# Recurrence layers: two products from GpSimd to VectorE, and the split of the output put at places of its own

## The chip, the cores and the metric

The kernel runs on one core of a Trainium2 chip. The metric is device microseconds of one execution. Before the change the median of three runs is 1669.04 us (1668.2 to 1670.75). Names used below: TensorE (PE; PEld is its weight load), VectorE (DVE), ScalarE (ACT), GpSimd (POOL), SyncE (SP, which issues the transfers). SBUF is the on-chip memory that tiles live in, PSUM the banks that matmuls write.

## The reference

One step of a network with four layers over 384 tokens (128 of a prompt, 256 of a sample) with 1024 features. Layers 0 and 3 mix tokens with a gated linear recurrence in both directions, layer 1 with a short gated convolution, layer 2 with pooling; each layer also has an MLP, layer norms and modulation. The part that matters:

```python
def rglru_direction(xc, w_a, b_a, w_x, b_x, lam, h0, reverse):
    xb = xc.reshape(bsz, T, N_LRU_BLOCKS, LRU_BLOCK)
    r = jax.nn.sigmoid(jnp.einsum('btnd,nde->btne', xb, w_a).reshape(bsz, T, D_RNN) + b_a)
    ig = jax.nn.sigmoid(jnp.einsum('btnd,nde->btne', xb, w_x).reshape(bsz, T, D_RNN) + b_x)
    log_a = (-LRU_C * r.astype(jnp.float32)) * jax.nn.softplus(-lam.astype(jnp.float32))
    a = jnp.exp(log_a)
    u = jnp.sqrt(-jnp.expm1(2.0 * log_a)) * (ig * xc).astype(jnp.float32)
    ...
    h, h_last = linear_recurrence(a, u, h0.astype(jnp.float32))      # h[t] = a[t] h[t-1] + u[t]

def lru_mixer(x, w_in, conv_w, conv_b, w_a, b_a, w_x, b_x, lam, w_out, h0):
    gate, rec = jnp.split(x @ w_in, 2, axis=-1)
    xc = depthwise_conv(rec, conv_w, LRU_PAD_L, LRU_PAD_R) + conv_b
    h_f, s_f = rglru_direction(xc, ..., h0[:, 0], False)
    h_b, s_b = rglru_direction(xc, ..., h0[:, 1], True)
    y = jax.nn.gelu(gate) * (h_f + h_b).astype(x.dtype)
    return y @ w_out, jnp.stack([s_f, s_b], axis=1).astype(x.dtype)
```

## The kernel before

**Tiling.** Features lie on the 128 partitions, in 8 chunks, and the tokens on the free axis. A tile of 388 columns is the 384 tokens with gaps between the two groups; 776 columns are both directions of one chunk. Every large product is done in three matmuls for each 128 x 128 tile of weights: weights and inputs are split into a rounded high half (hi, `whi`) and the remainder (lo, `wlo`), and L197, L198 and L199 multiply hi by hi, lo by hi and hi by lo into one PSUM bank (`acc`). Weights arrive as `raw`; ScalarE makes `whi` (L1279) and VectorE `wlo` (L1285), 1024 columns, that is eight tiles, at a time. There are four such pairs of buffers, and a split is made three half blocks ahead.

**Order.** The program is written out as a list of weight tiles. After each tile there is one tick, and `defer(n, fn)` issues a piece of work n ticks later (a tile of three matmuls on TensorE is one tick). From the program written in this order a scheduler of the language then sets the order of each engine's instructions, gives out the eight PSUM banks and the buffers, and adds the waits. Each engine runs its own list strictly in order, so an instruction that waits holds all behind it.

**A recurrence layer.** The input product has 16 output chunks. Eight are the recurrence's: each is convolved by one ScalarE step (L875) and three VectorE steps (L879), all reading the PSUM bank. Eight are the output's gate: ScalarE squares (L993), VectorE makes a polynomial (L996), ScalarE a tanh (L999), VectorE the product (L1000, the last to read the bank). Between them stand four sets of gates, `gates(g)`, for chunks 2g and 2g+1: eight matmuls at full fp32, each in two passes (L893), with a tanh on ScalarE behind each (L895). Behind a set, `chain(g)` defers for its two chunks, each with ticks of its own: `s_p` (VectorE, L916), `s_tau` (two tanh, ScalarE, L930), `s_sqrt` (root on ScalarE, L933, and a product on GpSimd, L934), `s_a` (two exponentials, ScalarE, L941), `s_u` (VectorE L945, then GpSimd fills the gaps, L947 and L948), `s_scan` (two scans on VectorE, L953 and L956), `s_sum` (GpSimd: a fill, the sum of both directions L962, and two copies of the last states, L964 and L965), and `s_y` (VectorE L970, the gated output, then hi on ScalarE, L236, and lo on VectorE, L237). The output product (L197 to L199 on `hid`) takes chunks 0 to 5 first for five of its outputs, and then 6 and 7.

ScalarE's functions come in sets: where root follows tanh or exponential, an `ACT_TABLE_LOAD` stands between.

The names: `hidf` and `lru` are buffers of the chain (a ring of ten for gates, tau and a) and of the layer's scratch, `tmp` a pool of short-lived tiles, `hid` the split halves that the output product reads, `st` the states, `par` the parameters.

Of the kernel before, what the change touches and what calls it, by code (L numbers as in the profile page):

```python
# [11 lines left out]
F32 = mybir.dt.float32  # L12
F32R = mybir.dt.float32r
I32 = mybir.dt.int32
AF = mybir.ActivationFunctionType
ALU = mybir.AluOpType
# [15 lines left out]
LG = 388  # L32
# [98 lines left out]
def backbone_kernel(ctx, tc, xT, par, wmod0, wmodp, wmodv, w1, w2, lin, lgate, lout, scin, scout, poolw, y_out, st_out):  # L131
    nc = tc.nc
    act, vec, gp, pe = nc.scalar, nc.vector, nc.gpsimd, nc.tensor
# [19 lines left out]
    def tmp(n=T):  # L153
        return tmpp.tile([P, LB], F32, tag="tmp", name=nm("tmp"))[:, :n]
# [27 lines left out]
    def defer(n, fn):  # L182
        seq[0] += 1
        heapq.heappush(heap, (tickno[0] + n, seq[0], fn))
# [50 lines left out]
    def split_hi_lo(src, hi, lo, on_lo=None):  # L235
        act.activation(hi, src, AF.Copy)  # L236
        (on_lo or vec).tensor_tensor(lo, src, hi.bitcast(F32), op=ALU.subtract)  # L237
# [39 lines left out]
    def lru_col(t, j, c, d):  # L277
        i = (j * C + c) * 2 + d
        return t[:, i : i + 1]
# [567 lines left out]
    def lru(l, j, ng):  # L847
        S = {}
# [15 lines left out]
        def buf():  # L864
            ring[0] += 1
            return S["ring"][ring[0] % len(S["ring"])][:, : 2 * LG]
# [18 lines left out]
        def gates(g):  # L885
            def make(i):
                c, d, k = 2 * g + i // 4, (i // 2) % 2, i % 2

                def f(w):
                    if i % 4 == 0:  # L890
                        S["tr", c], S["ti", c] = buf(), buf()
                    ps = acc()[:, :LG]
                    pe.matmul(ps, lhsT=w, rhs=S["xc", c], start=True, stop=True)  # L893
                    dst = S[("tr", "ti")[k], c][:, d * LG : (d + 1) * LG]
                    act.activation(dst, ps, AF.Tanh, scale=0.5, bias=lru_col((bah, bxh)[k], j, c, d))  # L895
                    if i == 7:
                        chain(g)

                return f

            def block(raw):
                for i in range(8):
                    make(i)(raw[:, i * P : (i + 1) * P])
                    if i < 7:
                        tick()

            G(lgate[j, g], block)

        def chain(g):
            ca, cb = 2 * g, 2 * g + 1  # L910
            two = lambda t: t.rearrange("p (d t) -> p d t", d=2)
            gap = lambda t: two(t)[:, :, TP : TP + 3]

            def s_p(c):
                ti = S["ti", c]
                vec.scalar_tensor_tensor(  # L916
                    two(ti),
                    two(ti),
                    1.0,
                    S["xc", c].unsqueeze(1).to_broadcast([P, 2, LG]),  # L920
                    op0=ALU.add,
                    op1=ALU.mult,
                )

            def s_tau(c):
                S["tau", c] = buf()
                for d in range(2):
                    s = slice(d * LG, (d + 1) * LG)
                    cq = lru_col(c8q, j, c, d)
                    act.activation(S["tau", c][:, s], S["tr", c][:, s], AF.Tanh, scale=cq, bias=cq)  # L930

            def s_sqrt(c):
                act.activation(S["tau", c], S["tau", c], AF.Sqrt, scale=0.25)  # L933
                gp.tensor_tensor(S["ti", c], S["ti", c], S["tau", c], op=ALU.mult)  # L934

            def s_a(c):
                S["a", c] = buf()
                for d in range(2):
                    s = slice(d * LG, (d + 1) * LG)
                    ch = lru_col(c8h, j, c, d)  # L940
                    act.activation(S["a", c][:, s], S["tr", c][:, s], AF.Exp, scale=ch, bias=ch)  # L941

            def s_u(c):
                a, u = S["a", c], S["ti", c]
                vec.scalar_tensor_tensor(u, a, 1.0, u, op0=ALU.add, op1=ALU.mult)  # L945
                e = PCOLS["edge"][0] + (j * C + c) * 6
                gp.memset(gap(a), 0.0)  # L947
                gp.tensor_copy(gap(u), two(par_t[:, e : e + 6]))  # L948

            def s_scan(c):  # L950
                a, u, h = S["a", c], S["ti", c], S["tr", c]
                n = LG - 1
                vec.tensor_tensor_scan(h[:, :n], a[:, :n], u[:, :n], 0.0, op0=ALU.mult, op1=ALU.add)  # L953
                hb = PCOLS["h0b"][0] + j * C + c
                rev = lambda t: t[:, LG : LG + n][:, ::-1]
                vec.tensor_tensor_scan(rev(h), rev(a), rev(u), par_t[:, hb : hb + 1], op0=ALU.mult, op1=ALU.add)  # L956

            def s_sum(c):
                h = S["tr", c]
                hs = tmp(LG)  # L960
                gp.memset(hs[:, LG - 1 :], 0.0)
                gp.tensor_tensor(hs[:, : LG - 1], h[:, : LG - 1], h[:, LG : 2 * LG - 1], op=ALU.add)  # L962
                i = j * 16 + c
                gp.tensor_copy(st[:, i : i + 1], h[:, TP - 1 : TP])  # L964
                gp.tensor_copy(st[:, i + 8 : i + 9], h[:, LG : LG + 1])  # L965
                S["hs", c] = hs

            def s_y(c):
                gg = S["gg", c]
                vec.scalar_tensor_tensor(gg, gg, 0.5, S["hs", c], op0=ALU.mult, op1=ALU.mult)  # L970
                hi, lo = S["y"][c]
                split_hi_lo(gg, hi, lo)

            for fn, da, db in (
                (s_p, 1, 2),
                (s_tau, 1, 3),
                (s_sqrt, 6, 6),
                (s_a, 10, 12),
                (s_u, 16, 18),
                (s_scan, 17, 19),  # L980
                (s_sum, 18, 20),
                (s_y, 22, 25),
            ):
                defer(da, lambda fn=fn: fn(ca))
                defer(db, lambda fn=fn: fn(cb))
# [306 lines left out]
    for it in items:  # L1292
# [14 lines left out]
        else:  # L1307
# [9 lines left out]
            hi, lo = wt[k]  # L1317
# [144 lines left out]
```

## Time and profile before

| | |
|---|---|
| median of 3 runs | 1669.04 us (1668.2 to 1670.75) |
| profiled execution, its own time | 1668.76 us |
| its span in the trace | 1667.0 us |
| mean granted clock of TensorE | 0.984 |
| first recurrence layer with its tail | 57 to 186 us of the span |
| second recurrence layer with its tail | 1249 to 1376 us of the span |

The rest of the execution's time over the span, 1.8 us, lies around it. A row of the timeline gives the start in us from the span's start, the time that the instruction or group took, the engine, the line, the operation, out<-in with shapes, how many were joined, and in brackets the idle time of that engine before the row and what ended it. A row of stretches gives its bounds and length, the busy time of PE, PEld, DVE, ACT and POOL with counts, the granted clock (1 is full), the DMA share and GB/s. The lines themselves stand with the prediction.

### The profile page before, as it was taken

What the parts mean: (1) busy time and instruction counts of PE and PEld (TensorE: products, weight loads), DVE (VectorE), ACT (ScalarE), POOL (GpSimd) and SP (SyncE); (2) the same over time, 40 slices, a digit from 0 to 9 for tenths busy, and PEclk for the clock granted to TensorE, in tenths of its full rate; (3) what the DMA queues carried; (4) which work ended last, traced back from release to release, by engine and by line L of the source; (5) the groups of instructions that cost most, each with busy time, mean ns of one, the idle gap of its engine ahead of it and who ended that gap; (6) DMA issues with size and microseconds to landing.
All of it is one profiled execution on the core that took longest, in us unless ns stands there. A gap on an engine that the chain in (4) does not pass through costs nothing.

```text
span 1667.0 us, 24422 instructions
## 1 busy us (share of the span) xinstructions
PE 1592.4 (96%) x9656; PEld 1507.4 (90%) x9656; DVE 1179.3 (71%) x1790; ACT 746.4 (45%) x1128; POOL 409.9 (25%) x477
## 2 busy tenths in 40 slices
PE   7989999999999999999996899999999889999996
PEld 6667899999999999999995699999988789999995
DVE  4777999787475569867647899687477888534544
ACT  3775652243353345324434553244259746423432
POOL 2235350002320046000055250000433354000043
PEclk9999999999999999999998999999999999999998
DMA  9767356556443535654533356556333343333321
GB/s 372 266 233 273 130 202 251 182 179 247 152 152 127 192 137 202 227 177 175 213 143 127 127 202 230 200 190 235 107 115 101 129 162 127 127 127 127 127 76 38
DMA packets 42163, 287.75 MB, mean 173 GB/s; under 512 B 4801, under 2 KB 6977, under 8 KB 8129
## 3 DMA queue, kind: packets, MB, share of 16 engines
q1 hardware_dynamic: 42048, 286.20, 48.0%
q8 instruction: 75, 1.23, 0.3%
q14 instruction: 40, 0.32, 0.1%
HBM read 284.59 MB, written 1.59 MB: 172 GB/s over the span
## 4 chain that ended last, share of the span: by engine, by line
PE 80%; DVE 10%; ACT 4%; POOL 2%; issue 2%; DMA 1%; SPq 0%; DVEq 0%; POOLq 0%; ACTq 0%
PE acc L197 26%; PE acc L199 25%; PE acc L198 25%; DVE wlo L1285 1%; ACT hidf L930 1%; DVE lru L879 1%; PE acc L453 1%; DMA raw<-in_wmod 1%; POOL tmp L962 1%; DVE hidf L945 1%; DVE X L570 1%; PE acc L893 1%; DVE hidf L956 1%; ACT hidf L933 1%; ACT L933 1%
## 5 line engine op out<-in xcount | busy, mean ns | idle before, releaser
L1285 DVE TENSOR_TENSOR wlo<-raw,whi 128x1024 fp32r<-128x1024 f32 x338 | 436.5, 1292 | 170.5 <-ACT whi L1279 169.3
L1279 ACT ACTIVATE whi<-raw 128x1024 fp32r<-128x1024 f32 x338 | 356.2, 1056 | 427.9 <-PE acc L199 351.2
L197 PE MATMUL acc<-h,whi 128*128 128x384 f32 (+2 forms) x1488 | 508.5, 342 | 18.4 <-ACT h L718 10.5
L198 PE MATMUL acc<-h,wlo 128*128 128x384 f32 (+2 forms) x1488 | 506.1, 340 | 0.0
L199 PE MATMUL acc<-h,whi 128*128 128x384 f32 (+2 forms) x1488 | 477.4, 341 | 3.2 <-POOL h L723 3.2
L197 PE MATMUL acc<-hid,whi 128*128 128x384 f32 (+1 forms) x1216 | 413.9, 340 | 3.1 <-ACT hid L236 3.1
L199 PE MATMUL acc<-hid,whi 128*128 128x384 f32 (+1 forms) x1216 | 410.8, 338 | 3.3 <-DVE hid L237 3.3
L198 PE MATMUL acc<-hid,wlo 128*128 128x384 f32 (+1 forms) x1216 | 409.9, 337 | 0.0
L197 PEld LDWEIGHTS acc<-h,whi 128*128 128x128 f32 x1488 | 281.9, 189 | 29.7 <-ACT h L718 11.6
L199 PEld LDWEIGHTS acc<-h,whi 128*128 128x128 f32 x1488 | 278.8, 189 | 6.4 <-POOL h L723 4.9
L198 PEld LDWEIGHTS acc<-h,wlo 128*128 128x128 f32 x1488 | 281.6, 189 | 1.5 <-issue 0.5
L197 PEld LDWEIGHTS acc<-hid,whi 128*128 128x128 f32 x1216 | 229.1, 188 | 8.3 <-ACT hid L236 4.3
L199 PEld LDWEIGHTS acc<-hid,whi 128*128 128x128 f32 x1216 | 229.1, 188 | 4.6 <-DVE hid L237 4.6
L198 PEld LDWEIGHTS acc<-hid,wlo 128*128 128x128 f32 x1216 | 228.9, 188 | 0.9
L830 ACT ACTIVATE tmp<-acc,par 128x384 f32<-128x384 f32 x128 | 74.2, 580 | 259.3 <-PE acc L199 259.3
L570 POOL TENSOR_TENSOR X<-X,ssb 128x384 f32<-128x384 f32 x49 | 55.7, 1172 | 484.3 <-ACT ssb L568 484.3
L547 DVE SCALAR_TENSOR_TENSOR X<-acc,m,X 128x128 f32<-128x128 f32 (+1 forms) x176 | 64.5, 410 | 127.1 <-PE acc L199 127.1
L446 DVE SCALAR_TENSOR_TENSOR mac<-macr,sil,mac 128x512 f32<-128x512 f32 x176 | 125.5, 747 | 0.0
L832 DVE TENSOR_TENSOR tmp<-tmp 128x384 f32<-128x384 f32 x128 | 71.7, 560 | 65.9 <-ACT tmp L830 65.8
L446 DVE SCALAR_TENSOR_TENSOR mac<-mac,sil 128x512 f32<-128x512 f32 x132 | 94.6, 752 | 0.0
L777 POOL TENSOR_SCALAR X<-X,ag,xbb 128x128 f32<-128x128 f32 x64 | 91.8, 1448 | 0.4
L420 POOL TENSOR_SCALAR sc<-m 128x16 f32<-128x16 f32 x7 | 3.5, 496 | 335.8 <-DVE m L384 335.4
(193 smaller groups left out, 1343.6 us busy)
## 6 DMA issues: line engine op xcount, KB each, us to landing
raw<-in_w SPq DMA_DIRECT2D x128, 1024.0 KB, 4.8
raw<-in_wmodp SPq DMA_DIRECT2D x26, 1024.0 KB, 4.9
macr<-in_wmodv SPq DMA_DIRECT2D x22, 1024.0 KB, 5.1
mac<-in_wmodv SPq DMA_DIRECT2D x22, 1024.0 KB, 4.9
park<-in_wmodp SPq DMA_DIRECT2D x18, 1024.0 KB, 8.2
raw<-in_lin SPq DMA_DIRECT2D x16, 1024.0 KB, 5.2
raw<-in_scin SPq DMA_DIRECT2D x12, 1024.0 KB, 4.8
raw<-in_wmod SPq DMA_DIRECT2D x8, 1024.0 KB, 7.4
```

Source lines behind the costliest of these rows:

```text
L197: pe.matmul(ps, lhsT=hi, rhs=xhi, start=first, stop=False)
L198: pe.matmul(ps, lhsT=lo, rhs=xhi, start=False, stop=False)
L199: late = lambda: pe.matmul(ps, lhsT=hi, rhs=xlo, start=False, stop=last)
L446: vec.scalar_tensor_tensor(a, x, w, a, op0=ALU.mult, op1=ALU.add)
L547: vec.scalar_tensor_tensor(Xt[c][:, o : o + n], ps[:, a:b], col(g, c, k), Xt[c][:, o : o + n], op0=ALU.mult, op1=ALU.add)
L570: (vec if fast and i > 2 else gp).tensor_tensor(Xt[i], Xt[i], ssb, op=ALU.subtract)
L777: gp.tensor_scalar(Xt[c][:, a:b], Xt[c][:, a:b], col(g, c, k), col(xb, c, k), op0=ALU.mult, op1=ALU.add)
L830: act.activation(r, ps[:, :T], AF.Relu, bias=par_t[:, i : i + 1])
L832: vec.tensor_tensor(q, r, r, op=ALU.mult)
L933: act.activation(S["tau", c], S["tau", c], AF.Sqrt, scale=0.25)
L1279: act.activation(hi, raws[id(raw)][:, i * 1024 : (i + 1) * 1024], AF.Copy)
L1285: vec.tensor_tensor(lo, raws[id(raw)][:, i * 1024 : (i + 1) * 1024], hi.bitcast(F32), op=ALU.subtract)
```

## The change

The product behind the root (L934) moves from GpSimd to VectorE and becomes a step of its own, `s_mul`, at ticks 12 and 14 for the two chunks; before it was issued right behind the root at tick 6. The sum of the two directions (L962) moves to VectorE. The exponentials go from ticks 10 and 12 to 9 and 11, `s_u` and `s_scan` to 17 and 21, `s_sum` and `s_y` to 18 and 22. Hi (`s_hi`) and lo (`s_lo`) of the output become steps of their own, four and six ticks behind `s_y`.

```diff
             def s_sqrt(c):
                 act.activation(S["tau", c], S["tau", c], AF.Sqrt, scale=0.25)
-                gp.tensor_tensor(S["ti", c], S["ti", c], S["tau", c], op=ALU.mult)
+
+            def s_mul(c):
+                vec.tensor_tensor(S["ti", c], S["ti", c], S["tau", c], op=ALU.mult)
...
-                gp.tensor_tensor(hs[:, : LG - 1], h[:, : LG - 1], h[:, LG : 2 * LG - 1], op=ALU.add)
+                vec.tensor_tensor(hs[:, : LG - 1], h[:, : LG - 1], h[:, LG : 2 * LG - 1], op=ALU.add)
...
                 vec.scalar_tensor_tensor(gg, gg, 0.5, S["hs", c], op0=ALU.mult, op1=ALU.mult)
+
+            def s_hi(c):
+                act.activation(S["y"][c][0], S["gg", c], AF.Copy)
+
+            def s_lo(c):
                 hi, lo = S["y"][c]
-                split_hi_lo(gg, hi, lo)
+                vec.tensor_tensor(lo, S["gg", c], hi.bitcast(F32), op=ALU.subtract)
...
                 (s_sqrt, 6, 6),
-                (s_a, 10, 12),
-                (s_u, 16, 18),
-                (s_scan, 17, 19),
-                (s_sum, 18, 20),
-                (s_y, 22, 25),
+                (s_a, 9, 11),
+                (s_mul, 12, 14),
+                (s_u, 17, 21),
+                (s_scan, 17, 21),
+                (s_sum, 18, 22),
+                (s_y, 18, 22),
+                (s_hi, 22, 26),
+                (s_lo, 24, 28),
```

Lines of the changed kernel: the product is L936, the exponentials L943, `s_u` L947 with its fills L949 and L950, the scans L955 and L958, the sum L964 with its copies L966 and L967, y L972, hi L975, lo L979; the gate of the output is L1003, L1006, L1009 and L1010, the splits of weights L1289 and L1295.

TensorE's and SyncE's lists keep their order; only VectorE's, ScalarE's and GpSimd's lists of the two recurrence layers differ. Three places. First, VectorE in the first layer, at the chain of the second set of gates (`acc_970` is the bank of a gate chunk, whose last reader is L1000 or L1010). Before, from the first `s_u` of this set:

```order
L945 SCALAR_TENSOR_TENSOR hidf_135<-hidf_140,hidf_135 128x776
L879 SCALAR_TENSOR_TENSOR lru_134<-acc_919,par,lru_134 128x388
L953 SCALAR_TENSOR_TENSOR lru_134<-hidf_140,hidf_135 128x387
L879 SCALAR_TENSOR_TENSOR lru_134<-acc_919,par,lru_134 128x388
L956 SCALAR_TENSOR_TENSOR lru_134<-hidf_140,par,hidf_135 128x387
L879 SCALAR_TENSOR_TENSOR lru_134<-acc_919,par,lru_134 128x388
L945 SCALAR_TENSOR_TENSOR hidf_137<-hidf_141,hidf_137 128x776
L1285 TENSOR_TENSOR wlo_980<-raw_820,whi_979 128x1024
L953 SCALAR_TENSOR_TENSOR hidf_136<-hidf_141,hidf_137 128x387
L956 SCALAR_TENSOR_TENSOR hidf_136<-hidf_141,par,hidf_137 128x387
L996 SCALAR_TENSOR_TENSOR tmp_1016<-tmp_1016,acc_970 128x388
L970 SCALAR_TENSOR_TENSOR lru_134<-lru_134,tmp_1008 128x388
```

Now, in the same place, behind the product L936, a lo, the L947 and the two scans of chunk 2g+1, which now come first:

```order
L879 SCALAR_TENSOR_TENSOR lru_134<-acc_919,par,lru_134 128x388 x3
L936 TENSOR_TENSOR hidf_135<-hidf_135,hidf_138 128x776
L1295 TENSOR_TENSOR wlo_979<-raw_820,whi_978 128x1024
L947 SCALAR_TENSOR_TENSOR hidf_135<-hidf_140,hidf_135 128x776
L1006 SCALAR_TENSOR_TENSOR tmp_1014<-tmp_1014,acc_970 128x388
L955 SCALAR_TENSOR_TENSOR lru_134<-hidf_140,hidf_135 128x387
L958 SCALAR_TENSOR_TENSOR lru_134<-hidf_140,par,hidf_135 128x387
L964 TENSOR_TENSOR tmp_1041<-hidf_136 128x387
L964 TENSOR_TENSOR tmp_1005<-lru_134 128x387
L972 SCALAR_TENSOR_TENSOR lru_134<-lru_134,tmp_1041 128x388
L972 SCALAR_TENSOR_TENSOR lru_134<-lru_134,tmp_1005 128x388
L1010 SCALAR_TENSOR_TENSOR lru_134<-tmp_1015,acc_970 128x388
```

The two chunks have changed places, both products and both sums have come in, one weight split and the lo's stand elsewhere.

Second, ScalarE at the same place (`hidf_138` and `hidf_139` are tau of the two chunks). Before:

```order
L933 ACT_TABLE_LOAD
L933 ACTIVATE hidf_138<-hidf_138 128x776
L933 ACTIVATE hidf_139<-hidf_139 128x776
L875 ACTIVATE lru_134<-acc_919,par 128x388
L941 ACT_TABLE_LOAD
```

Now:

```order
L933 ACT_TABLE_LOAD
L933 ACTIVATE hidf_139<-hidf_139 128x776
L975 ACTIVATE hid_127<-lru_134 128x388
L930 ACT_TABLE_LOAD
L930 ACTIVATE hidf_138<-lru_134,c8q 128x388 x2
L875 ACTIVATE lru_134<-acc_919,par 128x388
L933 ACT_TABLE_LOAD
L933 ACTIVATE hidf_138<-hidf_138 128x776
```

The two roots, side by side before, have the tanh of the first chunk between them now, with two more table loads. It is the only set where this happens.

Third, VectorE at the tail of the first layer, chunks 6 and 7 (`hid_132` and `hid_133`). Before:

```order
L945 SCALAR_TENSOR_TENSOR lru_134<-hidf_137,lru_134 128x776
L1285 TENSOR_TENSOR wlo_1446<-raw_1273,whi_1445 128x1024
L953 SCALAR_TENSOR_TENSOR hidf_142<-hidf_137,lru_134 128x387
L956 SCALAR_TENSOR_TENSOR hidf_142<-hidf_137,par,lru_134 128x387
L970 SCALAR_TENSOR_TENSOR lru_134<-lru_134,tmp_1435 128x388
L1285 TENSOR_TENSOR wlo_1490<-raw_1273,whi_1489 128x1024
L237 TENSOR_TENSOR hid_132<-lru_134,hid_132 128x388
L970 SCALAR_TENSOR_TENSOR lru_134<-lru_134,tmp_1451 128x388
L1285 TENSOR_TENSOR wlo_1522<-raw_1313,whi_1521 128x1024
L237 TENSOR_TENSOR hid_133<-lru_134,hid_133 128x388
```

Now:

```order
L947 SCALAR_TENSOR_TENSOR lru_134<-hidf_137,lru_134 128x776
L972 SCALAR_TENSOR_TENSOR lru_134<-lru_134,tmp_1432 128x388
L955 SCALAR_TENSOR_TENSOR hidf_142<-hidf_137,lru_134 128x387
L958 SCALAR_TENSOR_TENSOR hidf_142<-hidf_137,par,lru_134 128x387
L1295 TENSOR_TENSOR wlo_1442<-raw_1274,whi_1441 128x1024
L964 TENSOR_TENSOR tmp_1460<-hidf_142 128x387
L979 TENSOR_TENSOR hid_132<-lru_134,hid_132 128x388
L972 SCALAR_TENSOR_TENSOR lru_134<-lru_134,tmp_1460 128x388
L1295 TENSOR_TENSOR wlo_1489<-raw_1274,whi_1488 128x1024
L979 TENSOR_TENSOR hid_133<-lru_134,hid_133 128x388
```

The y of chunk 6 stands ahead of the scans of chunk 7, and its lo ahead of chunk 7's y; the sum L964 has come in, and one of the three weight splits stands further up.

## The prediction

> **What bounds the kernel now.** I read the page first, then the busy time of the first recurrence layer, then the idle times of TensorE, then what VectorE, GpSimd and ScalarE did ahead of each.
>
> ```profile
> PE 1592.4 (96%) x9656; PEld 1507.4 (90%) x9656; DVE 1179.3 (71%) x1790; ACT 746.4 (45%) x1128; POOL 409.9 (25%) x477
> PE 80%; DVE 10%; ACT 4%; POOL 2%; issue 2%; DMA 1%; SPq 0%; DVEq 0%; POOLq 0%; ACTq 0%
> 57.00:186.00 129.00, 116.61 (x693) 92.42 (x696) 98.22 (x140) 86.38 (x132) 52.63 (x68) 0.97 0.64 233
> ```
>
> TensorE is the bound. The last row is the first recurrence layer (stretch, length, busy time of PE, PEld, DVE, ACT, POOL, granted clock): of 129 us TensorE is idle 12.4, and VectorE has only 31 free. The change can only win back idle time and lowered clock in the two such layers, and adds work to the engine that is nearly full there. The idle time sits in a few places; in the first layer in two.
>
> Place 1, the third set of gates (two TensorE rows, then a row of the stretch behind, with the granted clock third from its end):
>
> ```profile
> 99.92 3.53 PE L893 MATMUL acc<-lru,raw 128*128 128x388 f32 x10
> 107.66 3.50 PE L893 MATMUL acc<-lru,raw 128*128 128x388 f32 x6 [4.21 <-DVE lru L1000]
> 108.00:112.00 4.00, 4.00 (x18) 1.63 (x20) 3.94 (x8) 4.00 (x9) 0.00 (x0) 0.57 0.43 104
> ```
>
> A gate is two passes, so the first row is five gates. The sixth needs the PSUM bank that L1000 on VectorE reads last, and waits 4.21 us; the clock then drops. Why is L1000 late? VectorE, GpSimd and ScalarE:
>
> ```profile
> 93.54 2.60 DVE L945 SCALAR_TENSOR_TENSOR hidf<-hidf,hidf 128x776 f32<-128x776 f32 x1 [2.51 <-POOL hidf L934]
> 96.07 0.61 DVE L879 SCALAR_TENSOR_TENSOR lru<-acc,par,lru 128x388 f32<-128x388 f32 x1
> 96.60 0.95 DVE L953 TENSOR_TENSOR_SCAN lru<-hidf,hidf 128x387 f32<-128x387 f32 x1
> 97.47 0.59 DVE L879 SCALAR_TENSOR_TENSOR lru<-acc,par,lru 128x388 f32<-128x388 f32 x1
> ...
> 105.45 1.21 DVE L1285 TENSOR_TENSOR wlo<-raw,whi 128x1024 fp32r<-128x1024 f32 x1
> 106.58 0.55 DVE L237 TENSOR_TENSOR hid<-lru,hid 128x388 fp32r<-128x388 f32 x1
> 107.06 0.54 DVE L1000 SCALAR_TENSOR_TENSOR lru<-tmp,acc 128x388 f32<-128x388 f32 x1
> ```
> ```profile
> 91.61 3.71 POOL L934 TENSOR_TENSOR hidf<-hidf,hidf 128x776 f32<-128x776 f32 x2 [5.94 <-ACT hidf L933]
> ```
> ```profile
> 89.39 1.28 ACT L933 ACT_TABLE_LOAD   x1
> 90.68 1.59 ACT L933 ACTIVATE hidf<-hidf 128x776 f32<-128x776 f32 x2
> 104.50 0.53 ACT L999 ACTIVATE tmp<-tmp 128x388 f32<-128x388 f32 x1 [6.76 <-DVE tmp L996]
> ```
>
> VectorE stands 2.51 us for the product on GpSimd, then its own L945 takes 2.60 us while GpSimd's second product runs; alone the same form takes 0.94 (row at 149.75 below). From 93.54 on VectorE is never free, and ScalarE waits 6.76 us for it.
>
> Place 2, the tail: the output product needs hi and lo of the last two chunks.
>
> ```profile
> 155.98 0.44 PE L197 MATMUL acc<-hid,whi 128*128 128x388 f32 x1 [1.24 <-ACT hid L236]
> 157.84 0.44 PE L199 MATMUL acc<-hid,whi 128*128 128x388 f32 x1 [1.24 <-DVE hid L237]
> 158.87 0.44 PE L197 MATMUL acc<-hid,whi 128*128 128x388 f32 x1 [0.59 <-ACT hid L236]
> 159.92 0.69 PE L199 MATMUL acc<-hid,whi 128*128 128x388 f32 x1 [0.43 <-DVE hid L237]
> 160.00:164.00 4.00, 4.00 (x13) 3.56 (x14) 1.97 (x3) 1.50 (x2) 0.00 (x0) 0.62 1.01 414
> 149.75 0.94 DVE L945 SCALAR_TENSOR_TENSOR lru<-hidf,lru 128x776 f32<-128x776 f32 x1
> 153.03 0.96 DVE L953 TENSOR_TENSOR_SCAN hidf<-hidf,lru 128x387 f32<-128x387 f32 x1 [1.21 <-POOL lru L948]
> 149.91 2.80 POOL L962 TENSOR_TENSOR tmp<-hidf 128x387 f32<-128x387 f32 x1
> 155.40 0.53 ACT L236 ACTIVATE hid<-lru 128x388 fp32r<-128x388 f32 x1 [5.57 <-DVE lru L970]
> ```
>
> The sum L962 on GpSimd takes 2.80 us beside VectorE, holds up the fill L948 behind it, and so the scan.
>
> The second recurrence layer has the same pattern, at four sets and the tail:
>
> ```profile
> 1275.72 0.45 PE L197 MATMUL acc<-h,whi 128*128 128x392 f32 x1 [0.97 <-DVE lru L1000]
> 1293.38 2.85 PE L893 MATMUL acc<-lru,raw 128*128 128x388 f32 x8 [0.23 <-issue]
> 1298.18 2.19 PE L893 MATMUL acc<-lru,raw 128*128 128x388 f32 x6 [1.95 <-DVE lru L879]
> 1301.64 0.92 PE L893 MATMUL acc<-lru,raw 128*128 128x388 f32 x2 [1.27 <-ACT lru L895]
> 1303.95 0.70 PE L197 MATMUL acc<-h,whi 128*128 128x392 f32 x1 [1.39 <-ACT hidf L895]
> 1323.23 2.87 PE L893 MATMUL acc<-lru,raw 128*128 128x388 f32 x8 [0.83 <-DVE lru L879]
> 1302.00:1310.00 8.00, 6.61 (x21) 6.05 (x20) 6.86 (x11) 7.93 (x15) 0.00 (x0) 0.57 0.66 216
> 1284.26 1.59 ACT L933 ACTIVATE hidf<-hidf 128x776 f32<-128x776 f32 x2
> 1287.10 2.60 DVE L945 SCALAR_TENSOR_TENSOR hidf<-hidf,hidf 128x776 f32<-128x776 f32 x1 [5.12 <-POOL hidf L934]
> 1347.02 0.44 PE L197 MATMUL acc<-hid,whi 128*128 128x388 f32 x1 [0.71 <-ACT hid L236]
> 1348.88 0.44 PE L199 MATMUL acc<-hid,whi 128*128 128x388 f32 x1 [1.24 <-DVE hid L237]
> 1351.00:1355.00 4.00, 4.00 (x12) 3.56 (x13) 1.97 (x3) 1.35 (x2) 0.00 (x0) 0.58 0.40 158
> ```
>
> **The change, part by part.** The product L934 as it stands on GpSimd (form, count, busy time, mean ns, idle time before):
>
> ```profile
> L934 POOL TENSOR_TENSOR hidf<-hidf,hidf 128x776 f32<-128x776 f32 x10 | 18.5, 1869 | 54.5 <-ACT hidf L933 54.5
> ```
>
> GpSimd loses 16 of these and 16 of L962. VectorE has no row of the 776-wide product; between the 388-wide L237 (start to next start 0.48) and the 1024-wide L1285 (1.13), both products of two SBUF operands, a line gives 0.88; the ends 0.48 and 1.22 bound it. The sum is as wide as L237: 0.48. So VectorE takes on 16 x 1.36 = 21.8 us over the two layers, 2.7 per set of gates. It loses the stretching: L945 drops from 2.60 to 0.94 where GpSimd's product ran beside it, and the waits for GpSimd of 2.51 and 5.12 go.
>
> Contention does not vanish: GpSimd keeps fills and state copies. [...]
>
> Place 1. The compiled order changes: the root of the set's second chunk comes first on ScalarE, then a rounding, then a table load, two tanh, a conv start and a second table load before the other root: two loads more in the program, here only. The first root ends between 89.8 and 91.5 (before: 90.68 plus half of 1.59); I take 90.6. The second: 0.43 + 1.28 + 1.2 + 0.56 + 1.28 + 0.8 = 5.5 later, 96.1. VectorE from 90.6 to the end of the gate's last step (L1010, formerly L1000): two products 1.76, two of the old L945 1.76, four scans 3.6, three conv steps 1.6, one split 1.13, and two sums, two y, one lo, one poly, one L1010 at 0.47 each, 3.3: 13.1 us. The second product is reached at 96.2, so its root costs nothing; 0.4 goes on GpSimd's fill before the first scan. That is 104.1, with hand-offs at most 105.5; I take 105.0 against 107.60. Gain 2.6, and if the clock holds, (1 - 0.57) x 4 = 1.7 more: 4.3 (from 0 to 5.3). The loads run on ScalarE beside VectorE's backlog.
>
> [...]
>
> Place 2. Hi and lo now stand at separate ticks, and the scan no longer waits for L962 and its fill. In the old time scale the last scan starts at 149.75 + 0.85 (L947) + 0.47 (y) = 151.1, and behind it stand two scans 1.8, split 1.13, sum, lo, y at 0.47, split 1.13, lo 0.55: the last lo at 157.1, the last hi at 156.0. TensorE without stalls wants them at 156.4 and 155.8. Chunk 6 is ready long before. The fill behind L947 costs nothing, since the y stands between. Left: 0.7 of 3.5, gain 2.8 (1 to 3.5), and the clock's (1 - 0.62) x 4 = 1.5 (0 to 1.5). First layer: -8.6.
>
> Second layer. Second set: the 0.97 goes, since L945's stretch ahead of L1000 goes. Third set: the roots begin at 1284.26 now, and with the 0.97 and a lighter queue ahead of them the first ends at about 1283.5. VectorE then has, up to the last of the six conv steps (L879) that this set waits for, two products 1.76, one old L945 0.88, the fill 0.35, two scans 1.8, six conv steps 3.2, a split 1.13, a sum and a y 0.96: 10.1, that is 1293.6. The second half of the set wants it at 1293.38 - 1.0 + 2.85 = 1295.2, so the 1.95 goes and the two waits behind it with it: sixteen passes of 0.345 from 1293.38 end at 1298.9 instead of 1303.95, 5.0. Clock: (1 - 0.57) x 8 = 3.4, less as TensorE stood 1.4 of the stretch; 3.0. Fourth set: VectorE is late in turn. From 1283.5 some 18 us of its work stand before this set's chain can go on (to 1301), and ScalarE's rounding of chunk 5, which waits for a y in that queue, stands ahead of the last two tanh, and so of the next roots. I get waits of 0.9 and 1.85 where 0.83 was: +1.9 (0 to 4, with a lost clock). Tail: with the last two waits as in the first layer it loses 0.71 + 1.24 + 0.59 + 0.43 = 3.0; VectorE being later here, I leave 1.4: 1.6 gained, and (1 - 0.58) x 4 = 1.7. Together 1.0 + 5.0 + 3.0 - 1.9 + 1.6 + 1.7 = 10.4.
>
> Edits at no cost: the exponentials, one tick earlier, run in ScalarE's free time. The weight splits (L1285) stand behind more VectorE work, but are made three half blocks ahead, and the product that reads the low half never waits now:
>
> ```profile
> L198 PE MATMUL acc<-h,wlo 128*128 128x384 f32 (+2 forms) x1488 | 506.1, 340 | 0.0
> ```
>
> That cover would be gone if VectorE fell some 10 us behind. SP's transfers keep their order. GpSimd's fills and copies now stand behind nothing long. Other layers are unchanged.
>
> Sum: 8.6 + 10.4 = 19.0 off the profiled execution's 1668.76 (0.28 under the median of 1669.04): 1649.8. I say **1650**.
>
> **Rivals.**
> A, part of it. The clock stays low at the third set of the second layer (+3.0) and falls at its fourth, where 2.75 us of waits come close together (+2 to +3), or place 1's L1010 stays near 107: 1655 to 1661. For it: place 2 lost its clock after 3.5 us of scattered waits. [...]
> B, only the tails gain (2.8 + 1.5 + 1.6 + 1.7 = 7.6): 1661. Needs VectorE's new 2.7 per set to use up all that the stretch gives back.
> C, the change does not do what it says: rounding set later keeps the output waiting as before and the new waits cancel the gates' gain: about 1668. Against it: in the compiled order chunk 6's lo stands ahead of chunk 7's y.
> D, slower. VectorE becomes the gate: no relief from GpSimd's remaining copies, and 2.7 us of new work lie ahead of the conv steps and L1010 at three sets, 8.1, plus the two loads 2.6: 1679. It decides if the old L945 still takes above 1.4 us and L1010 ends after 107.6.
>
> **How the numbers follow.** Forecast 0.62 (own range 1644 to 1655), A 0.22, B 0.05, C 0.05, D 0.06. The range 1644 to 1661 leaves out C, D and a little of both ends. 0.2% (3.3 us) is what a measurement of this kernel can tell from no change. Faster 0.89, same 0.05, slower 0.06.
>
> **What would show it.** Right: the old L945 at 0.95 everywhere; the third set of the first layer with a wait near 1.6 and no clock under 1; at the tail one wait of some 0.7; the second layer's third set without a wait over 0.5. Wrong: ScalarE's roundings (L975) standing for VectorE ahead of the tanh of the gates, or conv steps (L879) releasing the gates late in more than the fourth set.

## The result, and the profile after

| | before | after |
|---|---|---|
| median of 4 runs each | 1669.22 us (1668.2 to 1670.75) | 1649.66 us (1649.31 to 1650.79) |
| profiled execution, its own time | 1668.76 | 1649.62 |
| its span | 1667.0 | 1647.8 |
| mean granted clock | 0.984 | 0.989 |

The ratio is 0.9882 with a 95% interval of 0.9869 to 0.9894: 1.2% faster, 19.6 us. The forecast was 1650.

The page of the changed kernel, busy times and chain:

```profile
PE 1583.4 (96%) x9656; PEld 1501.8 (91%) x9656; DVE 1188.8 (72%) x1822; ACT 749.8 (46%) x1130; POOL 362.7 (22%) x445
PE 80%; DVE 12%; ACT 4%; issue 2%; POOL 1%; DMA 1%; SPq 0%; DVEq 0%; POOLq 0%; ACTq 0%
```

GpSimd has 47 us less, but VectorE has only 9.5 us more, although rows of 24.3 us came to it (16 of L936 with 15.4 in sum, 16 of L964 with 8.9). In part its other rows got shorter: L945's sixteen take 15.4 us in sum where they took 21.5, the y's 2.4 less and the weight splits 2.8 less. In part it is counting: rows that follow one another directly overlap by some 0.09 us in the records, and the busy time counts that once. TensorE's busy time fell by 9.0 with the same instructions; by an estimate from the two clocks, 0.989 of full speed over the span instead of 0.984, about 8 of it go with the granted clock (0.005 of 1592.4). The two recurrence layers as stretches (bounds as before, moved with the work):

```profile
55.00:179.00 124.00, 117.93 (x722) 93.41 (x725) 107.33 (x166) 92.29 (x138) 29.64 (x52) 0.99 0.67 249
1240.00:1357.00 117.00, 109.88 (x558) 96.97 (x560) 104.55 (x149) 91.53 (x141) 25.68 (x49) 1.00 0.39 140
```

VectorE is now busy 107 of 124 and 105 of 117 us, GpSimd less than 30. By lines, the moved product (L936) and the old L945 (L947 now), and the sum (L964) on VectorE:

```profile
L936 DVE TENSOR_TENSOR hidf<-hidf,hidf 128x776 f32<-128x776 f32 x10 | 9.4, 962 | 7.6 <-ACT hidf L933 7.6
L947 DVE SCALAR_TENSOR_TENSOR hidf<-hidf,hidf 128x776 f32<-128x776 f32 x10 | 9.6, 964 | 5.4 <-ACT hidf L943 5.4
L964 DVE TENSOR_TENSOR tmp<-hidf 128x387 f32<-128x387 f32 x12 | 6.6, 553 | 0.0
```

The product takes 0.96 us here and 1.87 on GpSimd. L947 takes 0.964 on average where L945 took 1.501, with the same shape and inputs. It waits for the exponentials only; no wait for GpSimd is left in it. Over the two layers VectorE's waits for GpSimd fall from 10.6 to 1.2 us. GpSimd's one-column copies of the last states still read SBUF beside VectorE. They take 0.18 us at the least and up to 2.52, while none of VectorE's L936 and L947 takes more than 0.97; the forecast's sum has no term for them.

Places 1 and 2 of the prediction, TensorE:

```profile
102.23 4.18 PE L893 MATMUL acc<-lru,raw 128*128 128x388 f32 x12
106.79 1.90 PE L893 MATMUL acc<-lru,raw 128*128 128x388 f32 x4 [0.38 <-DVE lru L1010]
...
152.50 0.44 PE L197 MATMUL acc<-hid,whi 128*128 128x388 f32 x1 [0.30 <-ACT hid L975]
153.55 0.44 PE L199 MATMUL acc<-hid,whi 128*128 128x388 f32 x1 [0.44 <-DVE hid L979]
```

The 4.21 us has become 0.38, and the tail's four waits (3.5 us) two of 0.74 together. The clock stays at 1 behind both:

```profile
106.00:110.00 4.00, 3.56 (x24) 1.40 (x23) 4.00 (x8) 3.70 (x9) 0.37 (x3) 1.00 0.67 225
152.00:156.00 4.00, 2.89 (x14) 1.96 (x12) 4.00 (x6) 1.51 (x2) 0.00 (x0) 1.00 0.48 131
```

The second layer:

```profile
1260.91 5.38 PE L893 MATMUL acc<-lru,raw 128*128 128x388 f32 x16
1283.29 5.38 PE L893 MATMUL acc<-lru,raw 128*128 128x388 f32 x16
1303.05 2.85 PE L893 MATMUL acc<-lru,raw 128*128 128x388 f32 x8 [1.51 <-ACT whi L1289]
1307.59 2.87 PE L893 MATMUL acc<-lru,raw 128*128 128x388 f32 x8 [1.69 <-DVE lru L879]
...
1331.72 0.45 PE L197 MATMUL acc<-hid,whi 128*128 128x388 f32 x1 [0.53 <-ACT hid L975]
1332.77 0.45 PE L199 MATMUL acc<-hid,whi 128*128 128x388 f32 x1 [0.42 <-DVE hid L979]
```

The second and third sets run through. The fourth has two new waits. The first of them is put down to a split of weights on ScalarE; VectorE's rows show what really came last:

```profile
1297.79 0.97 DVE L936 TENSOR_TENSOR lru<-lru,hidf 128x776 f32<-128x776 f32 x1 [1.01 <-ACT hidf L933]
1298.67 0.96 DVE L936 TENSOR_TENSOR hidf<-hidf,hidf 128x776 f32<-128x776 f32 x1
...
1302.36 0.60 DVE L879 SCALAR_TENSOR_TENSOR lru<-acc,par,lru 128x388 f32<-128x388 f32 x1
```

The third conv step of the chunk ends at 1302.96, and the gates that read its result start at 1303.05.

Where the 19.2 us between the two spans lie, by the starts of the same matmuls in both traces (after minus before, then the step from the line above):

| place | after - before | step |
|---|---|---|
| first product of layer 0 (44.40, 45.49) | +1.09 | +1.09 |
| second set of gates (76.59, 79.38) | +2.79 | +1.70 |
| third set (99.92, 102.23) | +2.31 | -0.48 |
| fourth set (128.93, 126.05) | -2.88 | -5.19 |
| behind the first tail (188.92, 181.70) | -7.22 | -4.34 |
| first set of layer 3 (1250.29, 1241.81) | -8.48 | -1.26 |
| third set of layer 3 (1293.38, 1283.29) | -10.09 | -1.61 |
| its fourth set (1319.63, 1303.05) | -16.58 | -6.49 |
| behind its tail (1372.48, 1353.34) | -19.14 | -2.56 |

Some of these steps do not come from the change. The first 1.09 begins with the first transfer, for which the first matmul waits 9.74 us instead of 8.44. The 1.70 behind it is a difference of clock behind a wait that is the same in both: 1.84 us for L879, with a clock of 1.00 behind it in before and of 0.50 for 3.41 us in after. The -1.26 lies in layers whose code is the same. In the traces of this case (that with the fills left out) the first product of layer 0 starts between 44.4 and 47.3 us, and the stretch from behind the first tail to the first set of layer 3 takes 1060.0 to 1062.9, so a difference of 2 us between two executions need not come from an edit.

```profile
63.08 2.85 PE L893 MATMUL acc<-lru,raw 128*128 128x388 f32 x8 [1.84 <-DVE lru L879]
```
```profile
64.18 4.54 PE L893 MATMUL acc<-lru,raw 128*128 128x388 f32 x8 [1.84 <-DVE lru L879]
```

### The profile page after: what moved, and what is told of

The parts are those of the page before. It is cut to its first block, busy times and chain, and to the rows that moved or that the text cites. A ratio compares the mean times of both kernels' runs of the same rounds, so it can differ in the third digit from the quotient of the medians.

```text
span 1647.8 us, 24431 instructions
## 1 busy us (share of the span) xinstructions
PE 1583.4 (96%) x9656; PEld 1501.8 (91%) x9656; DVE 1188.8 (72%) x1822; ACT 749.8 (46%) x1130; POOL 362.7 (22%) x445
## 4 chain that ended last, share of the span: by engine, by line
PE 80%; DVE 12%; ACT 4%; issue 2%; POOL 1%; DMA 1%; SPq 0%; DVEq 0%; POOLq 0%; ACTq 0%
PE acc L197 26%; PE acc L199 25%; PE acc L198 25%; DVE wlo L1295 2%; DVE lru L879 1%; DMA raw<-in_wmod 1%; ACT hidf L930 1%; PE acc L453 1%; DVE X L570 1%; DVE hidf L958 1%; DVE X L547 1%; ACT L933 1%; ACT hidf L933 1%; DVE X L659 1%; POOL h L723 1%
## 5 line engine op out<-in xcount | busy, mean ns | idle before, releaser
L1295 DVE TENSOR_TENSOR wlo<-raw,whi 128x1024 fp32r<-128x1024 f32 x338 | 433.7, 1284 | 168.0 <-ACT whi L1289 166.7
L1289 ACT ACTIVATE whi<-raw 128x1024 fp32r<-128x1024 f32 x338 | 356.1, 1056 | 428.1 <-PE acc L199 351.7
L197 PE MATMUL acc<-h,whi 128*128 128x384 f32 (+2 forms) x1488 | 507.6, 341 | 16.0 <-ACT h L718 10.5
```

Source lines behind the costliest of these rows:

```text
L197: pe.matmul(ps, lhsT=hi, rhs=xhi, start=first, stop=False)
L1289: act.activation(hi, raws[id(raw)][:, i * 1024 : (i + 1) * 1024], AF.Copy)
L1295: vec.tensor_tensor(lo, raws[id(raw)][:, i * 1024 : (i + 1) * 1024], hi.bitcast(F32), op=ALU.subtract)
```

## The experiments

The question was which part of the change makes the gain and by what mechanism. Theory M: taking the products off GpSimd does it, because GpSimd's instructions stretch VectorE's beside them and because VectorE waits for GpSimd's results. Rival P: the new places do it. All kernels below were timed against before; the ratio and interval are against before's runs on the same chip.

| kernel | median us | ratio to before, 95% |
|---|---|---|
| both products moved, old places | 1654.74 | 0.991 (0.9896 to 0.9923) |
| new places, both products on GpSimd | 1669.28 | 0.9999 (0.9991 to 1.0008) |
| whole change, product on GpSimd | 1660.18 | 0.9938 (0.9924 to 0.9951) |
| whole change, sum on GpSimd | 1663.31 | 0.9967 (0.9954 to 0.9979) |
| whole change, and an unused product on GpSimd | 1662.18 | 0.9957 (0.9945 to 0.9969) |
| whole change, and an unused sum on GpSimd | 1664.42 | 0.9967 (0.9958 to 0.9977) |
| both moved, old places, hi and lo later | 1653.13 | 0.9904 (0.9891 to 0.9917) |
| whole change, hi and lo at y | 1654.21 | 0.991 (0.9895 to 0.9925) |
| sum on GpSimd, hi and lo later still | 1665.21 | 0.9969 (0.9957 to 0.9981) |
| whole change, hi and lo two ticks earlier | 1651.61 | 0.9893 (0.988 to 0.9907) |
| whole change, conv of chunk 1 earlier | 1648.42 | 0.9876 (0.9863 to 0.989) |
| whole change, fills on GpSimd | 1654.27 | 0.9914 (0.9899 to 0.9929) |

**Only the engines.** Before, with two words changed and every step at its old place.

```diff
-                gp.tensor_tensor(S["ti", c], S["ti", c], S["tau", c], op=ALU.mult)
+                vec.tensor_tensor(S["ti", c], S["ti", c], S["tau", c], op=ALU.mult)
...
-                gp.tensor_tensor(hs[:, : LG - 1], h[:, : LG - 1], h[:, LG : 2 * LG - 1], op=ALU.add)
+                vec.tensor_tensor(hs[:, : LG - 1], h[:, : LG - 1], h[:, LG : 2 * LG - 1], op=ALU.add)
```

> Both products on VectorE, but every step at its old place, hi and lo right behind y. Theory M (the gain comes from taking the products off GpSimd: the waits for L934, the stretch of L945 beside it, and the fill that waits behind L962): the gates of the third sets gain nearly as in the whole change, the tails about half: 1652 to 1657 us. Rival P (the gain comes from the new places; the moves alone only load VectorE): 1664 us or more.

1654.7 us: 14.2 of the 19.6 us, as M said. All sixteen rows of L945 take 0.94 to 0.97 us, at their old places. The second layer's fourth set pays for it in this version, with a wait of 4.00, behind which eight passes take 5.54 us where 2.85 is usual:

```profile
1311.01 5.54 PE L893 MATMUL acc<-lru,raw 128*128 128x388 f32 x8 [4.00 <-DVE lru L879]
```

**Only the places.** The whole change with both products on GpSimd (`gp` in both lines).

> All the new places, but both products stay on GpSimd. M: the product comes six ticks later on GpSimd and still stretches VectorE, so the gates' waits stay or grow; only the tails can gain: 1661 to 1670 us. P: 1650 to 1656 us.

1669.3 us: no change at all. Waits moved: the tail of the first layer still waits 2.53 us for hi, and the second layer's fourth set starts with a wait of 4.85. P falls.

```profile
160.95 0.45 PE L197 MATMUL acc<-hid,whi 128*128 128x388 f32 x1 [2.53 <-ACT hid L975]
...
1320.62 8.03 PE L893 MATMUL acc<-lru,raw 128*128 128x388 f32 x16 [4.85 <-ACT tmp L1003]
```

**One product at a time.** The whole change with one of the two `vec` lines back on `gp`.

> The whole change, but the product behind the root stays on GpSimd (at its new ticks 12 and 14). M: the wait for it and the stretch of the old L945 come back, the tails keep their gain: 1657 to 1665 us. P: 1650 to 1653 us.

> The whole change, but the sum of the directions stays on GpSimd. M: the gates keep their gain and the tails lose about half, as the fill for the last scan stands behind the sum again and y waits for the sum: 1652 to 1656 us. P: 1649 to 1651 us. If VectorE's load were what limits the changed kernel, taking 7.7 us off it would make it faster: under 1648 us.

The product back on GpSimd costs 10.5 us, inside M's range. The sum back costs 13.7, far more than either theory said. It was expected to matter at the tails alone, and a VectorE with less to do did not make the kernel faster either. With the product back, VectorE waits 7.5 us in all for it, and L947 takes up to 2.59 us again. With the sum back, the trace shows it holding the gates too: ScalarE's tanh L930 waits 4.37 us for it at the fourth set of the first layer, since it writes into the ring buffer that the sum reads, and the gates' L895 stand behind L930.

```profile
133.93 0.71 ACT L930 ACTIVATE lru<-hidf,c8q 128x388 f32<-128x388 f32 x1 [4.37 <-POOL tmp L964]
```
```profile
135.16 0.92 PE L893 MATMUL acc<-lru,raw 128*128 128x388 f32 x2 [2.31 <-ACT hidf L895]
```

The compiled lists of VectorE and ScalarE also differ from the changed kernel's in these two versions, so their differences are not the product alone.

**The products' work without their results.** To part M's two halves, GpSimd gets the work and nobody uses the result. VectorE's, ScalarE's and TensorE's compiled lists are those of the changed kernel, instruction for instruction, and GpSimd's has only the added instructions.

```diff
                 act.activation(S["tau", c], S["tau", c], AF.Sqrt, scale=0.25)
+                gp.tensor_tensor(dose, S["tau", c], S["tau", c], op=ALU.mult)
```

> The changed kernel, with one product more on GpSimd behind each root: it reads the same tau as before's L934, 776 wide, and writes a tile that nobody reads. Nobody waits for it. If the two engines exclude each other at SBUF (theory M's half that explains L945's 2.60), VectorE's rows beside it take up to 1.8 us more, 16 times, three or four of them on the path: 1653 to 1660 us. If only the wait for GpSimd's result mattered: 1649 to 1651 us.

1662.2 us, 12.5 more than the changed kernel, and in the trace no instruction stood waiting for the added one. GpSimd's small fills come later behind it, which is little: VectorE's waits for GpSimd are 2.3 us where they were 1.2. It costs about as much as putting the real product back. VectorE's rows show why (L938 is L936, L949 is L947; the dose is L935):

```profile
L938 DVE TENSOR_TENSOR hidf<-hidf,hidf 128x776 f32<-128x776 f32 x10 | 15.8, 1609 | 7.6 <-ACT hidf L934 7.6
L949 DVE SCALAR_TENSOR_TENSOR hidf<-hidf,hidf 128x776 f32<-128x776 f32 x10 | 13.5, 1352 | 1.2 <-ACT hidf L945 1.1
L935 POOL TENSOR_TENSOR dose<-hidf 128x776 f32<-128x776 f32 x14 | 28.5, 2038 | 67.0 <-ACT hidf L934 66.3
```

1.61 and 1.35 us where the changed kernel has 0.96. The rows above, with two inputs in SBUF, are stretched, while VectorE's conv steps (L880 here), which read one of their two tiles from PSUM, are not. Beside two doses in a row:

```profile
1306.97 2.25 DVE L938 TENSOR_TENSOR hidf<-hidf,hidf 128x776 f32<-128x776 f32 x1
1309.14 0.61 DVE L880 SCALAR_TENSOR_TENSOR lru<-acc,par,lru 128x388 f32<-128x388 f32 x1
1309.67 1.71 DVE L949 SCALAR_TENSOR_TENSOR lru<-hidf,lru 128x776 f32<-128x776 f32 x1
```
```profile
1306.20 4.36 POOL L935 TENSOR_TENSOR dose<-hidf 128x776 f32<-128x776 f32 x2 [8.32 <-ACT hidf L934]
```

The conv step at 1290.73, with nothing on GpSimd, takes 0.61 us as well. The dose stands beside other rows of VectorE than L934 did in before, so it shows that such work costs this much, and not what share of the 19.6 us is the stretch.

The same for the sum:

```diff
                 vec.tensor_tensor(hs[:, : LG - 1], h[:, : LG - 1], h[:, LG : 2 * LG - 1], op=ALU.add)
+                gp.tensor_tensor(dose[:, : LG - 1], h[:, : LG - 1], h[:, LG : 2 * LG - 1], op=ALU.add)
```

> The changed kernel, with the sum made a second time on GpSimd (387 wide, same inputs, into a tile nobody reads) behind VectorE's own. With the sum on GpSimd alone the kernel takes 1663.3 us. If its cost there is GpSimd's reading beside VectorE: 1656 us or more here. If it is that y, hi and the next tanh wait for GpSimd's result: 1649 to 1654 us here.

1664.4 us: 14.8 more, against 13.7 for the real sum on GpSimd. So the wait for the sum's result is not needed to explain its cost. Part of it is stretching: VectorE's own sum, side by side with its double, goes from 0.553 to 1.034 us.

```profile
L965 DVE TENSOR_TENSOR tmp<-hidf 128x387 f32<-128x387 f32 x12 | 12.4, 1034 | 0.0
```

Part is the ring: one tanh (L930, L931 here) waits 2.71 us for the dose, which reads the buffer too, and ScalarE waits 1.3 us more for state copies that stand behind the dose. And at the first tail VectorE's list has no slack: its sum takes 1.35 us beside the dose, and TensorE waits 3.02 us for lo, where it waited 0.44.

```profile
155.28 1.83 POOL L966 TENSOR_TENSOR dose<-hidf 128x387 f32<-128x387 f32 x1 [0.17 <-DVE hidf L959]
```
```profile
156.16 1.35 DVE L965 TENSOR_TENSOR tmp<-hidf 128x387 f32<-128x387 f32 x1
```
```profile
158.05 0.44 PE L199 MATMUL acc<-hid,whi 128*128 128x388 f32 x1 [3.02 <-DVE hid L981]
```

How much of the 14.8 us is each is not settled.

**Work that reads nothing.** Three fills on GpSimd behind each root in place of the dose.

```diff
                 act.activation(S["tau", c], S["tau", c], AF.Sqrt, scale=0.25)
+                for _ in range(3):
+                    gp.memset(dose, 0.0)
```

> The changed kernel, with three fills of a 776-wide tile on GpSimd behind each root in place of the product of the earlier run (1662.2 us): GpSimd works but reads nothing from SBUF. If VectorE's two-input instructions are blocked only by a GpSimd instruction that reads: 1649 to 1652 us, VectorE's rows at their lone times. If any work on GpSimd blocks them: 1655 us or more.

The time tells nothing on the question. A fill waits for nothing, and the scheduler put all 48 at the start, from 1.2 to 54.8 us, so none ran beside the recurrence. Of the 4.6 us more, 3.4 are a wait of 3.92 where 0.50 was, ahead of the first product. ScalarE's rounding of layer 0's input (L719) stands there for small fills of that tile's gaps, which lie on GpSimd behind the added ones:

```profile
49.76 0.69 PE L197 MATMUL acc<-h,whi 128*128 128x392 f32 x1 [3.92 <-ACT h L719]
```

The start of the same trace answers the question even so. Two pairs of weight splits (L1298 here) run there beside the added fills (L936 here), the second split of each pair wholly so:

```profile
17.69 2.36 DVE L1298 TENSOR_TENSOR wlo<-raw,whi 128x1024 fp32r<-128x1024 f32 x2 [0.32 <-ACT whi L1292]
...
29.14 2.36 DVE L1298 TENSOR_TENSOR wlo<-raw,whi 128x1024 fp32r<-128x1024 f32 x2
```
```profile
18.34 3.95 POOL L936 MEMSET dose<- 128x776 f32 x5
...
29.33 5.58 POOL L936 MEMSET dose<- 128x776 f32 x7
```

The same two pairs in the changed kernel, without the fills, take 2.36 us as well. Beside the dose that reads, a single split took 2.50:

```profile
100.66 2.50 DVE L1297 TENSOR_TENSOR wlo<-raw,whi 128x1024 fp32r<-128x1024 f32 x1
```

So a GpSimd that only writes left VectorE's rows with two inputs alone, in these places. It did not leave all of VectorE alone: two rows of L701, which read one tile, take 0.96 us beside the fills (at 44.98) and 0.67 without (at 26.32, and at 44.03 in the changed kernel).

**Hi and lo.** Three kernels on theory S: that hi, waiting for y in ScalarE's list, holds the tanh behind it.

```diff
-                (s_hi, 22, 26),
-                (s_lo, 24, 28),
+                (s_hi, 18, 22),
+                (s_lo, 18, 22),
```

> The whole change, but hi and lo at the ticks of y (18 and 22), as before the change relative to y. S: ScalarE waits for y again, the gates' waits grow: 1652 to 1657 us. If separate places of hi and lo do nothing: 1649 to 1651 us.

1654.2 us, 4.6 worse than the change. But not where S said: the third and fourth sets show about the change's waits (1.68 and 1.69 in the second layer, where the change has 1.51 and 1.69). It is the tails, 1.61 where 0.53 was in the second layer and above all the first layer's, where chunk 7's hi waits for its y and TensorE for it:

```profile
154.47 0.45 PE L197 MATMUL acc<-hid,whi 128*128 128x388 f32 x1 [3.48 <-ACT hid L975]
```

The second of these kernels has both products on VectorE at the old places, a product step at the old tick 6, and hi and lo four and six ticks behind y:

```diff
+                (s_mul, 6, 6),
                 (s_y, 22, 25),
+                (s_hi, 26, 29),
+                (s_lo, 28, 31),
```

> Both products on VectorE at the old places (1654.7 us with hi and lo right behind y), but hi four and lo six ticks behind y. Theory S (hi, waiting for y in ScalarE's queue, holds the tanh of the gates behind it): 1649 to 1653 us. If the other new places make the rest of the change's gain: 1654 to 1656 us.

1653.1 us against 1654.7 without; the intervals overlap, so it tells nothing on its own. The wait of 4.00 at the fourth set of the second layer is there as without.

```diff
-                (s_hi, 22, 26),
-                (s_lo, 24, 28),
+                (s_hi, 26, 30),
+                (s_lo, 28, 32),
```

> The whole change with the sum on GpSimd (1663.3 us at the changed places), but hi and lo two and four ticks later still for the first chunk and the second (hi 26 and 30, lo 28 and 32). S: hi no longer waits for a y that waits for the sum, most of the 13.6 us come back: 1653 to 1658 us. If VectorE's own wait for the sum (7.2 us in nine places) and its stretch are the loss: 1661 us or more.

The ticks are four later each, not as that text has it. 1665.2 us: nothing came back. S fails for the sum; the dose points to stretch and buffers. At the first layer's tail hi waits 4.87 us for y.

**Two variants.** Hi at 20 and 24, lo at 22 and 26, with 20 table loads instead of 22:

> The whole change, but hi two and lo four ticks behind y (20 and 24, 22 and 26). In the compiled order the chunks of the second set no longer change places, and the two table loads go. If the swap and the loads cost place 1 something: 1647 to 1649 us. If they are covered by VectorE's list, as predicted: 1649 to 1651 us; if hi then waits for y on ScalarE, 1651 to 1654 us.

1651.6 us: no better, and the interval overlaps the changed kernel's. It does not decide what the loads cost. In its trace the third set of the first layer has no wait, and the stretch from there to the fourth set is 0.97 us shorter than in the changed kernel. Against that, the stretch behind it with the first tail is 1.0 longer, and the layers behind that, with the same code, 2.2. What the swap and the two loads cost stays open; these two traces leave room for 0.97 us.

```diff
-            defer(5 if c == 1 else 1, conv)
+            defer(2 if c == 1 else 1, conv)
```

> The changed kernel, with the conv steps of chunk 1 issued two ticks behind the chunk instead of five, so that in the first layer they stand ahead of the weight split. The first set of gates waits 1.84 us there for L879 in both kernels, and the clock sometimes falls behind it. If that wait is on the path: 1645 to 1648 us. If the split of weights is then late: 1650 us or more.

1648.4 us, just above the range for a wait on the path. The 1.84 wait is gone, and so is the 0.74 at the first set of the second layer. It is the lowest median of all and beats before clearly; against the changed kernel (0.9876 and 0.9882 with overlapping intervals) it cannot be told apart.

## Why the prediction was right

The bound, the two engines and the places were right, and the sum came out within a microsecond: 19.0 forecast, 19.6 measured between the medians and 19.2 between the two spans. By its terms, forecast and then measured from the table of steps:

- The product's price, 0.88 from start to next start by interpolation: the rows behind L936 start 0.87 and 0.88 after it (92.85 to 93.72, 1297.79 to 1298.67). The stretch of L945 goes entirely, as said; its sixteen rows take 0.93 to 0.97. One row was misread on the way: the L945 at 149.75, taken as alone, has L962 on GpSimd beside it from 149.91. It kept its 0.94, and the sum, which started second, grew to 2.80 where 1.00 is its least. The price was right all the same.
- Place 1, 4.3: measured 5.19. The step that was mis-sized is the place of the wait: I kept it at the sixth gate. In the changed kernel the bank that L1010 reads last goes to the seventh (twelve passes, then the wait), two passes or 0.7 us later, so 0.38 is left where about 1.6 was forecast. The other 0.6 of that: in the old time scale (2.31 us less) the first root ended at 89.7 and not at 90.6, and L1010 at 104.4 and not at 105.0. The sequence itself held: the first root ends at 92.03 and L1010 at 106.73, 14.7 us against 14.4. The second root (ends 97.80) is ready before VectorE reaches its product at 99.17: the two loads are hidden, and the loads took 1.28 with the next row right behind, as before.

```profile
95.65 1.28 ACT L933 ACT_TABLE_LOAD   x1
96.95 0.86 ACT L933 ACTIVATE hidf<-hidf 128x776 f32<-128x776 f32 x1
```

- Place 2, 4.3: measured 4.34, with the last lo wanted 0.44 late.
- Second layer, 10.4: 1.6 + 6.5 + 2.6 = 10.7. The second set 1.0 forecast; the third with its clock and the first new wait 5.0 + 3.0 - 0.9 = 7.1, measured 6.5; the fourth and the tail 1.6 + 1.7 - 1.0 = 2.3, measured 2.6. The new waits of the fourth set were forecast as 0.9 and 1.85 and measured 1.51 and 1.69, and VectorE stands 1.01 us for the root there. The reason given for that wait did not hold: the rounding ahead of the last two tanh (L975 at 1290.90) waits for nothing. ScalarE stands 0.38 us for VectorE's polynomial just before, and from there to the root at 1296.90 it has no idle time to speak of.
- Rival A did not happen: the clock stayed up although waits of 1.51 and 1.69 us fell into these 8 us, and in the four other traces with two such waits (1.50 to 1.85 and 1.69 us) eight passes took 2.85 us behind the first and 2.87 behind the second, as here.

```profile
1302.00:1310.00 8.00, 5.26 (x16) 2.90 (x17) 7.92 (x12) 7.72 (x14) 1.40 (x4) 1.00 0.00 1
```

- What the prediction did not see: the other layers took 1.26 us less and the start 1.09 more with the same code, the clock behind the first set cost 1.70, and the stretch from the second set to the third gave 0.48. Together these cost 1.1 us, while the places of the forecast gave 20.2 instead of 19.0. That the two differences cancel to a fifth of a microsecond in this execution is luck; the places and most of their sizes are not. And the sum on GpSimd was costed at the tails alone; the experiments show that putting it back costs more than putting the product back (13.7 against 10.5 us), at the gates too. That need not hurt the forecast, since the waits at each place were read from VectorE's whole list and not from the single edit.
- One of the signs of being wrong did appear. ScalarE's rounding (L975) stands for VectorE ahead of the tanh of the gates at the third sets, 1.21 us at 106.30 and 1.97 at 1284.53. TensorE waits 0.38 us at the first of these sets and not at all at the second, so it cost next to nothing.

## What to carry to other kernels

Work moved from GpSimd to a VectorE that is already 76% busy in these layers can cost it much less than its own time: here rows of 24 us came in and 9.5 us of busy time were added, in part because L945, 1.50 us on average with the products on GpSimd, takes 0.96 without them. VectorE's waits for GpSimd went too, from 10.6 to 1.2 us. Test such a suspicion with work on the other engine that nobody waits for, and see that the compiled lists stay the same. New places alone gave nothing while both products stood on GpSimd (a ratio of 0.9999); behind the moves they were worth about 5 us (ratios of 0.991 and 0.9882, whose intervals just part).

## What the runs showed of the hardware

- A GpSimd product of 776 columns that reads SBUF, with no one waiting for it, raised VectorE's products of the same width from 0.96 to 1.61 us on average and cost 12.5 us in 16 times. GpSimd's own row was 2.04 there, against 1.87 in before.
- The same wait of 1.84 us left the clock at 1.00 in one execution and at 0.50 for 3.41 us in another, which cost 1.70 us.

```profile
61.19:64.61 3.42, 1.58 (x19) 0.74 (x19) 3.42 (x7) 1.76 (x3) 0.00 (x0) 1.00 1.00 405
64.61:68.02 3.41, 3.41 (x7) 1.86 (x6) 2.49 (x3) 1.84 (x3) 0.00 (x0) 0.50 0.99 396
```
```profile
60.67:64.08 3.41, 1.57 (x15) 0.77 (x8) 3.41 (x6) 1.32 (x3) 0.00 (x0) 1.00 1.02 408
64.08:67.50 3.42, 3.42 (x16) 2.69 (x15) 2.63 (x4) 3.39 (x7) 0.00 (x0) 1.00 1.02 417
```

The first two rows are of the changed kernel, the others of before. In each of these two traces all changes of the granted clock lie whole multiples of 3.413 us apart: in the changed kernel it falls at 64.61, 894.05 and 917.94 and is back at 68.02, 907.70 and 921.35; in before it falls at 108.46, 159.66 and 1303.12 and is back at 111.87, 163.07 and 1309.95, with the others on the same steps. Counted from the start of the span, the steps of the two executions do not coincide. The rows above run from step to step. They show that where the wait falls is not the whole of it, since in both executions it lies whole in one step, with 1.6 us of matmuls beside it. In the changed kernel 0.43 us of gates followed the wait in its step, and the clock fell; in before 1.00 us followed, and it stayed up. In other traces with this wait the eight passes behind it took 4.54 us with hi and lo two ticks earlier, and 2.84 or 2.85 with hi and lo at y, with the unused sum, and with the sum on GpSimd and hi and lo later still. Whether the order of wait and matmuls counts is not shown.
